# Late-used loads moved behind the first adaptive weights, and half of these weights put in operand slots, in a decoder trunk kernel

## Chip, core and metric

The kernel runs on one core of a Trainium2 chip. The metric is the device time of one launch in microseconds (us). A core has a tensor engine (PE, with its weight loads listed apart as PEld), a vector engine (DVE), a scalar engine (ACT), GpSimd (POOL), a sync engine (SP) that here issues nearly all loads, and 16 DMA engines that carry them out.

## What is computed

One sequence of 256 positions with 2048 features goes through two layers: an RWKV-7 time mix and a convolution module, each followed by a gated MLP. Each part is preceded by an RMS norm whose scale and shift come from a vector c. What bears on the change is the entry of the first layer:

```python
mod = silu(c) @ ada_w[0] + ada_b[0]          # 6 pieces of 2048: sh_m, sc_m, g_m, sh_f, sc_f, g_f
h  = rms_norm(x, g) * (1 + sc_m) + sh_m
xx = token_shift(h) - h
x_rkv = h + xx * mu[:3]                       # inputs of r, k, v
r, k, v = x_rkv @ w_rkv                       # three 2048 x 2048 products
xw, xa, xg = (h + xx * mu[n] for n in (3, 4, 5))
... tanh(xw @ w1), xa @ a1, sigmoid(xg @ g1)  # small inner products (widths 96, 96, 256)
```

Later stages use the rest of the parameters (biases, depthwise weights, gains), constant matrices, and silu(c) spread over all partitions for the other adaptive pieces, which the vector engine computes as row sums.

## The kernel before

Features lie on the 128 partitions, so a tensor of 2048 features is 16 tiles f = 0 to 15 of 128 x 256 positions. Weights come from memory in float32 in tiles of 128 x 2048 (1024 KB), and are split into a high and a low float32r part (`split_w`, L226: the high part by ACT at L231, the low by DVE at L232) for three matmuls each.

**Buffers.** Weights land in `raw_tile()`, a ring of four buffers. Operands live in `slot()`, a ring of 44 buffers of 2 x 260 columns; `slot512()` (L105) is one as a flat tile of 512 columns. The first stage fills the slots step by step: x takes 8, each tile leaves two operands and half of a third. The split weights have three buffers each.

**Head.** The sync queue first gets cb (c on all partitions, L168), all parameters par (L169), x in eight pieces (L332) and all constants cst (L333). ACT makes silu of cb; DVE makes three small derived vectors from par (L338 to L340); x is squared and summed for the norm.

**First stage**, lines 355 to 416. `ada_s(f)` computes scale and shift of tile f: it loads small weights lw (L359), then the adaptive weights in two halves `ada_s[f, 0]` and `ada_s[f, 1]`, each in a raw buffer (L364), for 16 matmuls with 32 columns (L367) into a PSUM tile of which one is free at a time, then loads the key weights w_k of tile f (L244). A copy on ACT (L371), two small products (L373) and two additions on DVE turn the sums into scale and shift. The loop then calls `ada_s(f + 1)`, scales tile f, mixes it with its shifted self for the different inputs, and makes ten key products with split weights (L398 to L400) and the inner products (L404 to L407). So a tile takes three raw buffers of the four: two halves and one w_k.

**What sets the order.** The code is traced; then a scheduler sorts the instructions of each engine's queue by its own estimate of readiness, and each queue runs in that order. A load that needs no buffer to come free can be placed far ahead of its place in the code. Buffers are handed out by the scheduler; a load into one waits until those who read its last content are done. The eight completion counters of loads are reused in turn, so a load also waits for the one eight places before it.

Of the kernel before, what the change touches and what calls it, by code (L numbers as in the profile page):

```python
# [14 lines left out]
ALU = mybir.AluOpType  # L15
# [65 lines left out]
SLAG = 2  # L81
BX = 2
CME = {mybir.EngineType.PE}
KAPPA = math.exp(-0.5)

_PCOLS = [
    ("gam_mix", 2 * KT), ("gam_ffn", 2 * KT), ("gam_fin", KT),
    ("ada_b", 2 * 6 * KT), ("c", KT), ("mu", 6 * KT),
    ("w0", KT), ("a0", KT), ("k_k", KT), ("k_a", KT), ("r_k", KT),
# [6 lines left out]
for _n, _w in _PCOLS:  # L96
    POFF[_n] = _o
    _o += _w
NPC = _o

_CCOLS = [("ident", P), ("bones", P), ("cen", P), ("ones", P), ("bo32", 32), ("sel", P),
          ("strict", T), ("incl", 2 * L), ("smask", T), ("eps", 4), ("e4", 1)]
COFF = {}
_o = 0
for _n, _w in _CCOLS:  # L105
    COFF[_n] = (_o, _w)
    _o += _w
NCC = _o


@with_exitstack
def trunk_kernel(ctx: ExitStack, tc: tile.TileContext, a, out):
# [24 lines left out]
    def raw_tile():  # L137
        return pool.tile([P, 2048], F32, tag="raw", bufs=4, name=nm("raw"))
# [22 lines left out]
    def act(o, i, func=AF.Identity, bias=0.0, scale=1.0):  # L161
        nc.scalar.activation(out=o, in_=i, func=func, bias=bias, scale=scale)  # L162

    # ---- constants, parameters
    cst = cp.tile([P, NCC], F32, name="cst")
    par = cp.tile([P, NPC], F32, name="par")
    cb = cp.tile([P, C], F32, name="cb")
    nc.sync.dma_start(out=cb, in_=a["cb"])  # L168
    nc.sync.dma_start(out=par, in_=a["par"])  # L169

# [4 lines left out]
    def pc(n, i=0, w=1):  # L175
        return par[:, POFF[n] + i:POFF[n] + i + w]
# [5 lines left out]

    act(cb, cb, AF.Silu)
    md = [cp.tile([P, 6 * KT], F32, name=f"md{i}") for i in range(2)]
# [37 lines left out]

    # ---- linear layers
    def split_w(r, k0, k1, step=1024, eng=None):
# [39 lines left out]
    class k_outer:  # L264
        """some outputs together, the operands fed one at a time; the weights split ahead, two operands' at once"""

# [39 lines left out]

    # ---- rms norm
    def sq_acc(st, x):
# [15 lines left out]

    # ================= layer 0: time mix =================
    hs = [slot() for _ in range(KT // 2)]
# [4 lines left out]
    for i in range(KT // 2):  # L331
        nc.sync.dma_start(out=hs[i][:, :, :T], in_=a["xT"][:, 2 * i:2 * i + 2, :])  # L332
    nc.sync.dma_start(out=cst, in_=a["cst"])  # L333
    st = [None]
# [3 lines left out]
    nc.vector.tensor_scalar(out=omu, in0=pc("mu", 0, 6 * KT), scalar1=-1.0, scalar2=1.0, op0=ALU.mult, op1=ALU.add)  # L338
    nc.vector.tensor_scalar(out=nkk_c, in0=pc("k_k", 0, KT), scalar1=-1.0, scalar2=None, op0=ALU.mult)
    nc.vector.tensor_scalar(out=oka, in0=pc("k_a", 0, KT), scalar1=-1.0, scalar2=1.0, op0=ALU.mult, op1=ALU.add)  # L340

    def xmix(n, f, t):
        act(t, hv(f), scale=omu[:, n * KT + f:n * KT + f + 1])
        stt(t[:, 1:T], hv(f)[:, 0:T - 1], pc("mu", n * KT + f), t[:, 1:T])
# [12 lines left out]
    def ada_s(f):  # L357
        lw = slot().rearrange("p a t -> p (a t)")[:, :448]
        nc.sync.dma_start(out=lw, in_=a["lw1"][f])  # L359
        # scale and shift of tile f  # L360
        pa = ps("y")
        for q in range(2):
            r = raw_tile()
            nc.sync.dma_start(out=r, in_=a["ada_s"][f, q])  # L364
            for k in range(8):
                g, kk = k % 4, 8 * q + k
                nc.tensor.matmul(pa[32 * g:32 * g + 32, :T], lhsT=cc[:, kk, :], rhs=r[:, k * T:(k + 1) * T],  # L367
                                 start=kk < 4, stop=kk >= 12, skip_group_check=True)
# [12 lines left out]
    for f in range(KT):  # L381
# [33 lines left out]
        xv32.append(xvp[-1][:, f % 2, :T])  # L415
        xmix(2, f, xv32[f])
    act(tw[:DL], lwa[:DL, :T], AF.Tanh)
    nc.scalar.copy(ta[:DL], lwa[:DL, T:])
# [17 lines left out]

    # ---- k, decay, a; A, B, K of the scan; N
    for f in range(KM, KT):
# [126 lines left out]

    # ---- inverse of the 32-blocks, all heads and chunks on partitions
    X = raw_tile()
# [65 lines left out]

    # ---- v, scan, group norm, bonus, gate
    def small(tag, w, bufs):
# [36 lines left out]
    def prep_gen(f):  # L672
# [7 lines left out]
        yield 0  # L680
        # products of A, R with B, K, and B, K by tokens
        for c in range(NC_):
# [12 lines left out]
            yield PU  # L695
        # off-diagonal block of the inverse
        py = ps("g")
# [5 lines left out]
        for h in range(2):  # L703
            r1 = slice(h * L + 32, h * L + 64)
            nc.scalar.copy(ysb[r1].rearrange("p c t -> p (c t)"), py[r1, :P])
        # bonus
        rk = t1()
# [6 lines left out]
        yield PU  # L714
        # centred V by tokens, in the other half of the partitions
        pvt = ps("g")
# [107 lines left out]

    # half of the output projection and residual, while the scan goes on
    def wo_gen(m):
# [34 lines left out]
    with tc.manual_schedule(engines={mybir.EngineType.PE}):  # L861
        while heap:
# [4 lines left out]
            if d is not None:  # L867
                at(t + d, g)
    # ---- output projection and residual
    # gain * x, with the shift in the last columns: the products of the two are rstd-free  # L870
    def operand(l, which, f):
# [29 lines left out]

    # ---- ConvGLU
    def ffn(l, st, ops, nops):
# [54 lines left out]

    # ================= layer 1: conformer convolution =================
    ops = nops  # L960
# [23 lines left out]

    # n of the taps on the tensor engine, m on GpSimd, the others on the vector engine in two chains
    def tap(f, d):
# [138 lines left out]

    # ---- final norm
    rstd = rstd_of(st)
# [108 lines left out]
```

## Time and profile before

| | us |
|---|---|
| median of 3 runs | 2667.47 |
| lowest, highest run | 2666.54, 2671.47 |
| span of the profiled execution | 2670.5 |
| PE busy in it | 2520.7 (94%) |
| DVE busy | 2003.9 (75%) |
| ACT busy | 1357.1 (51%) |

The profile is of one execution, whose span is the time from its first to its last instruction; a time of that execution beside its span is not listed. A busy PE need not be one at its peak. What is of use here are the first 200 us: how busy PE and the DMA engines are in stretches, what the sync queue waits for before it issues, how long a load takes from issue to landing, and the chain of work that ended last.

### The profile page before, as it was taken

The numbers are of one execution on the slowest core, as the hardware profiler recorded it, in microseconds if no ns is written. First come the engines' busy times: TensorE is split into PE (matmuls) and PEld (weight loads), VectorE is DVE, ScalarE is ACT, GpSimd is POOL, SyncE is SP. The second block draws the span as 40 slices with busy tenths as digits, with TensorE's granted clock in tenths as the row PEclk, the third lists the DMA queues.
The fourth block names the chain that finished last, engine by engine and source line by source line (L and its number), as shares of the span: only waits on it lengthen the run. The fifth ranks groups of instructions, "written<-read, shape, count | busy, mean of one in ns | idle before, by whom it ended". The sixth has DMA issues, their size and how long they took to land.

```text
span 2670.5 us, 52899 instructions
## 1 busy us (share of the span) xinstructions
PE 2520.7 (94%) x21250; PEld 2404.8 (90%) x21250; DVE 2003.9 (75%) x3635; ACT 1357.1 (51%) x2650; POOL 464.0 (17%) x452
## 2 busy tenths in 40 slices
PE   6899996999999999999999999978899999999998
PEld 3678885877799999999999999967899999999997
DVE  4567767768688888887878979979988656656665
ACT  4565622556555543553455555554555445534553
POOL 0000015544000012001100248954200000000000
PEclk9999997989999999999999999989999999999999
DMA  8887766677277778777978844436777655555553
GB/s 312 316 312 268 211 207 209 230 218 240 78 284 278 283 285 331 292 281 290 336 263 296 305 161 164 168 127 243 286 275 273 220 188 188 170 190 190 178 175 126
DMA packets 154805, 630.84 MB, mean 236 GB/s; under 512 B 60480, under 2 KB 72256, under 8 KB 95936
## 3 DMA queue, kind: packets, MB, share of 16 engines
q1 hardware_dynamic: 153824, 624.85, 65.9%
q8 instruction: 166, 2.72, 0.4%
q0 software_dynamic: 736, 2.62, 0.3%
q14 instruction: 79, 0.65, 0.1%
HBM read 614.30 MB, written 13.11 MB: 235 GB/s over the span
## 4 chain that ended last, share of the span: by engine, by line
PE 76%; DVE 10%; DMA 7%; ACT 3%; issue 2%; POOL 1%; SPq 0%; DVEq 0%; POOLq 0%; ACTq 0%
PE ps L237 22%; PE ps L239 22%; PE ps L238 21%; DMA raw<-ada 4%; DVE raw L208 3%; DVE s L159 2%; DVE lo L232 1%; PE ps L367 1%; PE ps L300 1%; DMA raw<-ada_s 1%; POOL lo L232 1%; DVE s L156 1%; PE ps L687 1%; ACT hi L231 1%; PE ps L398 1%
## 5 line engine op out<-in xcount | busy, mean ns | idle before, releaser
L237 PE MATMUL ps<-s,hi 128*128 128x258 f32 (+1 forms) x5584 | 1594.8, 286 | 7.5 <-ACT hi L231 6.4
L239 PE MATMUL ps<-s,lo 128*128 128x258 f32 (+1 forms) x5584 | 1581.6, 284 | 20.8 <-DVE lo L232 18.9
L238 PE MATMUL ps<-s,hi 128*128 128x258 f32 (+1 forms) x5584 | 1579.8, 283 | 0.6 <-DVE s L153 0.6
L231 ACT CAST hi<-raw 128x1024 fp32r<-128x1024 f32 (+6 forms) x873 | 769.7, 897 | 881.8 <-PE ps L238 606.1
L239 PEld LDWEIGHTS ps<-s,lo 128*128 128x128 f32 x5584 | 1063.7, 191 | 29.4 <-DVE lo L232 22.8
L237 PEld LDWEIGHTS ps<-s,hi 128*128 128x128 f32 x5584 | 1060.2, 190 | 16.8 <-ACT hi L231 8.6
L238 PEld LDWEIGHTS ps<-s,hi 128*128 128x128 f32 x5584 | 1063.4, 190 | 4.5 <-issue 3.0
L232 DVE TENSOR_TENSOR lo<-raw,hi 128x1024 fp32r<-128x1024 f32 (+4 forms) x639 | 746.0, 1171 | 303.5 <-ACT hi L231 301.8
L232 POOL TENSOR_TENSOR lo<-raw,hi 128x512 fp32r<-128x512 f32 x234 | 335.2, 1458 | 957.5 <-ACT hi L231 623.4
L208 DVE CUSTOM_DVE_ANT_0 raw<-raw,cb,par 128x1024 f32<-128x1024 f32 x156 | 213.2, 1367 | 76.0 <-DMA raw<-ada 71.3
L208 DVE CUSTOM_DVE_ANT_0 raw<-raw,cb,md 128x1024 f32<-128x1024 f32 x156 | 214.9, 1378 | 0.9
L159 DVE SCALAR_TENSOR_TENSOR s<-ps,par,s 128x239 f32<-128x239 f32 (+26 forms) x420 | 166.0, 456 | 1.8 <-ACT s L162 1.2
L1135 POOL TENSOR_TENSOR s<-s,t 128x256 f32<-128x256 f32 x6 | 4.1, 727 | 751.4 <-DVE t L322 751.4
L156 DVE TENSOR_TENSOR t<-ps,t 128x256 f32<-128x256 f32 x188 | 79.2, 422 | 47.5 <-PE ps L239 43.8
L159 DVE SCALAR_TENSOR_TENSOR s<-ps,md,s 128x256 f32<-128x256 f32 x117 | 55.9, 480 | 41.8 <-PE ps L239 41.7
L159 DVE SCALAR_TENSOR_TENSOR t<-t,par,t 128x255 f32<-128x255 f32 (+1 forms) x172 | 82.6, 480 | 1.9 <-ACT t L162 0.6
L156 DVE TENSOR_TENSOR s<-ps,cst 64x64 f32<-64x64 f32 (+2 forms) x208 | 48.1, 253 | 37.7 <-ACT n L689 27.0
L162 ACT ACTIVATE t<-t,par 128x256 f32<-128x256 f32 x118 | 68.1, 587 | 5.6 <-DVE t L156 2.5
L162 ACT ACTIVATE t<-t 128x256 f32<-128x256 f32 x102 | 42.5, 417 | 37.9 <-DVE t L159 24.1
L687 PE MATMUL ps<-s,s 128*128 128x128 f32 x256 | 46.6, 308 | 11.6 <-ACT s L694 10.6
L300 PE MATMUL ps<-s,raw 128*128 128x256 f32 x256 | 56.0, 380 | 0.0
L300 PEld LDWEIGHTS ps<-s,raw 128*128 128x128 f32 x256 | 48.4, 190 | 6.9 <-issue 0.3
(199 smaller groups left out, 2167.2 us busy)
## 6 DMA issues: line engine op xcount, KB each, us to landing
raw<-w_up SPq DMA_DIRECT2D x172, 1024.0 KB, 4.9
raw<-ada SPq DMA_DIRECT2D x156, 1024.0 KB, 6.7
raw<-w_dn SPq DMA_DIRECT2D x64, 896.0 KB, 4.7
raw<-w_pw SPq DMA_DIRECT2D x48, 1024.0 KB, 4.9
raw<-w_rkv SPq DMA_DIRECT2D x38, 1024.0 KB, 6.0
raw<-ada_s SPq DMA_DIRECT2D x32, 1024.0 KB, 6.4
raw<-w_dn SPq DMA_DIRECT2D x32, 960.0 KB, 4.9
raw<-w_o SPq DMA_DIRECT2D x11, 1024.0 KB, 4.9
```

The costliest lines, as they stand in the source:

```text
L156: nc.vector.tensor_tensor(out=o, in0=x, in1=y, op=ALU.mult)
L159: nc.vector.scalar_tensor_tensor(out=o, in0=x, scalar=s, in1=y, op0=op0, op1=op1)
L162: nc.scalar.activation(out=o, in_=i, func=func, bias=bias, scale=scale)
L208: nc.vector.tensor_tensor_reduce(out=r[q], in0=r[q], in1=cb[:, q * w:(q + 1) * w], scale=1.0, scalar=mod(l, piece, f) if q else pc("ada_b" ...
L231: nc.scalar.copy(hi[:, s], v[:, s])
L232: (eng or nc.vector).tensor_tensor(out=lo[:, s], in0=v[:, s], in1=hi[:, s], op=ALU.subtract)
L237: nc.tensor.matmul(acc[:, :n], lhsT=hi[:, c], rhs=x[:, 0, :n], start=first, stop=False)
L238: nc.tensor.matmul(acc[:, :n], lhsT=hi[:, c], rhs=x[:, 1, :n], start=False, stop=False)
L239: nc.tensor.matmul(acc[:, :n], lhsT=lo[:, c], rhs=x[:, 0, :n], start=False, stop=last)
L300: nc.tensor.matmul(acc[:, :T], lhsT=r[:, k * P:(k + 1) * P], rhs=hs32[k], start=k == 0, stop=k == n - 1)
L367: nc.tensor.matmul(pa[32 * g:32 * g + 32, :T], lhsT=cc[:, kk, :], rhs=r[:, k * T:(k + 1) * T], start=kk < 4, stop=kk >= 12, skip_group_che ...
L687: nc.tensor.matmul(pg[:, h * P:(h + 1) * P], lhsT=bkc, rhs=ari[h][:, c].rearrange("p j t -> p (j t)"), start=True, stop=True, skip_group_c ...
```

## The change

- The columns of par and cst are sorted anew, so that what the first stage uses stands first (336 of 1432 columns, 168 of 716 KB; 133 of 1317 columns, 66.5 of 658.5 KB). Only these are loaded at the head, and no cb.
- The rest of par and cst, and cb, are loaded by three instructions that stand in the code behind tile 13 of the first stage. The two derived vectors `nkk_c` and `oka` and the silu of cb stand behind the stage's loop.
- For tiles below SLF = 10, the second half of the adaptive weights goes to four slots of 512 columns, in four loads of 256 KB, instead of one raw buffer.

```diff
+SLF = 10
 _PCOLS = [
-    ("gam_mix", 2 * KT), ("gam_ffn", 2 * KT), ("gam_fin", KT),
-    ("ada_b", 2 * 6 * KT), ("c", KT), ("mu", 6 * KT),
+    ("gam_mix", 2 * KT), ("ada_b", 2 * 6 * KT), ("c", KT), ("mu", 6 * KT),
+    ("gam_ffn", 2 * KT), ("gam_fin", KT),
...
+NPE = POFF["gam_ffn"]
...
-    nc.sync.dma_start(out=cb, in_=a["cb"])
-    nc.sync.dma_start(out=par, in_=a["par"])
+    nc.sync.dma_start(out=par[:, :NPE], in_=a["par"][:, :NPE])
+    nc.sync.dma_start(out=cst[:, :NCE], in_=a["cst"][:, :NCE])
...
-    act(cb, cb, AF.Silu)
...
-    nc.sync.dma_start(out=cst, in_=a["cst"])
...
-            r = raw_tile()
-            nc.sync.dma_start(out=r, in_=a["ada_s"][f, q])
+            if q and f < SLF:
+                r = [slot512() for _ in range(4)]
+                for j in range(4):
+                    nc.sync.dma_start(out=r[j], in_=a["ada_s"][f, q][:, 2 * j * T:2 * (j + 1) * T])
+                r = [r[k // 2][:, (k % 2) * T:(k % 2 + 1) * T] for k in range(8)]
+            else:
+                r = raw_tile()
+                nc.sync.dma_start(out=r, in_=a["ada_s"][f, q])
+                r = [r[:, k * T:(k + 1) * T] for k in range(8)]
...
         xmix(2, f, xv32[f])
+        if f == KT - 3:
+            nc.sync.dma_start(out=par[:, NPE:], in_=a["par"][:, NPE:])
+            nc.sync.dma_start(out=cst[:, NCE:], in_=a["cst"][:, NCE:])
+            nc.sync.dma_start(out=cb, in_=a["cb"])
+    nc.vector.tensor_scalar(out=nkk_c, in0=pc("k_k", 0, KT), scalar1=-1.0, scalar2=None, op0=ALU.mult)
+    nc.vector.tensor_scalar(out=oka, in0=pc("k_a", 0, KT), scalar1=-1.0, scalar2=1.0, op0=ALU.mult, op1=ALU.add)
+    act(cb, cb, AF.Silu)
```

The order that the scheduler makes of it differs from the code's. In it the line numbers are those of each kernel: the issue of w_k is L244 before and L246 after, of ada_s L364 before, L369 (raw) and L365 (slot) after, of lw L359 and L358.

The sync queue of before, from the second half of tile 1 (`raw_213`) over the key weights of tile 1 (`raw_223`) and both halves of tile 2 (`raw_303`, `raw_313`) to the key weights of tile 3:

```order
L364 DMA raw_213<-ada_s 128x2048
L244 DMA raw_223<-w_k 128x1280
L364 DMA raw_303<-ada_s 128x2048
L364 DMA raw_313<-ada_s 128x2048
L244 DMA raw_323<-w_k 128x1280
L359 DMA s_300<-lw 128x448
L364 DMA raw_402<-ada_s 128x2048
L364 DMA raw_412<-ada_s 128x2048
L244 DMA raw_422<-w_k 128x1280
```

The same queue after, from the key weights of tile 1 (`raw_231`): first halves of tiles 2 and 3 are `raw_311` and `raw_416`, the first quarter of tile 2's second half is `s_321`, the two `l` are small weights of a later stage, which before stand two places ahead of `raw_213`:

```order
L246 DMA raw_231<-w_k 128x1280
L424 DMA par<-par 128x1096
L425 DMA cst<-cst 128x1184
L426 DMA cb<-cb 128x2048
L551 DMA l_418_2277<-lw 96x256
L551 DMA l_421_2285<-lw 96x256
L369 DMA raw_311<-ada_s 128x2048
L246 DMA raw_337<-w_k 128x1280
L369 DMA raw_416<-ada_s 128x2048
L358 DMA s_308<-lw 128x448
L365 DMA s_321<-ada_s 128x512
```

The three moved loads stand between tile 1 and tile 2, and the key weights of tile 2, the first half of tile 3 and lw of tile 2 have come ahead of the second half of tile 2.

The sync queue of before further on, with what each load waits for (PE, DVE: those that read the buffer's last content; DMAHW: the completion counters of loads): both halves of tile 6 are `raw_701` and `raw_711`, of tile 7 `raw_800` and `raw_810`:

```order
L364 DMA raw_701<-ada_s 128x2048 [waits DMAHW4_49,DMAHW1_49,PE_49]
L359 DMA s_598<-lw 128x448
L364 DMA raw_711<-ada_s 128x2048 [waits DMAHW2_49,PE_49]
L359 DMA s_698<-lw 128x448 [waits DMAHW7_49]
L244 DMA raw_721<-w_k 128x1280 [waits DMAHW0_49,DVE_49]
L364 DMA raw_800<-ada_s 128x2048 [waits DMAHW4_49,PE_49]
L364 DMA raw_810<-ada_s 128x2048 [waits DMAHW3_49,DVE_49]
L244 DMA raw_820<-w_k 128x1280 [waits DMAHW6_49,PE_49]
```

The same place after: key weights of tiles 6 and 7 are `raw_759` and `raw_864`, the first half of tile 7 is `raw_838`, the four quarters of tile 6's second half are `s_743` to `s_746`, the first half of tile 8 is `raw_944`:

```order
L246 DMA raw_759<-w_k 128x1280 [waits DMAHW2_49,PE_49]
L369 DMA raw_838<-ada_s 128x2048 [waits DMAHW3_49,DVE_49]
L246 DMA raw_864<-w_k 128x1280 [waits DMAHW4_49,PE_49]
L358 DMA s_730<-lw 128x448 [waits DMAHW5_49]
L365 DMA s_743<-ada_s 128x512 [waits DMAHW6_49]
L365 DMA s_744<-ada_s 128x512 [waits DMAHW7_49]
L365 DMA s_745<-ada_s 128x512 [waits DMAHW0_49]
L365 DMA s_746<-ada_s 128x512 [waits DMAHW1_49]
L369 DMA raw_944<-ada_s 128x2048 [waits DMAHW2_49,DVE_49]
```

The quarters wait for no buffer of their own, but stand behind the key weights of the next tile, which wait for PE; the buffer that these take is that of tile 6's first half.

The vector queue after, in tile 0 (`t_286` and `t_297` are mixes of it, `lo_353` is the low part of tile 1's key weights):

```order
L162 SCALAR_TENSOR_TENSOR t_286<-s_79,par,t_286 128x255
L427 TENSOR_SCALAR nkk_c<-par 128x16
L428 TENSOR_SCALAR oka<-par 128x16
L162 SCALAR_TENSOR_TENSOR t_297<-s_79,par,t_297 128x255
L234 TENSOR_TENSOR lo_353<-raw_231,hi_352 128x640
```

Before, `nkk_c` and `oka` were the second and third instruction of that queue; now they stand inside tile 0 and read the late part of par.

## Rows read from the trace of the kernel before

**Rows 1.** Busy time by stretch: engine columns in us with instructions, clock, DMA share, GB/s.

```profile
core 0: us, PE busy (x) PEld busy (x) DVE busy (x) ACT busy (x) POOL busy (x), PEclk, DMA share, GB/s
0.00:20.00 20.00, 2.31 (x14) 1.18 (x18) 7.87 (x19) 10.95 (x21) 0.73 (x5) 1.00 0.94 344
...
38.00:45.00 7.00, 7.00 (x57) 4.83 (x58) 0.83 (x2) 1.45 (x2) 0.00 (x0) 1.00 0.00 1
50.00:170.00 120.00, 106.58 (x939) 81.84 (x938) 61.78 (x159) 66.07 (x150) 0.00 (x0) 0.96 0.88 321
190.00:210.00 20.00, 20.00 (x170) 19.94 (x169) 16.02 (x22) 8.58 (x13) 0.00 (x0) 1.00 0.90 332
```

**Rows 2.** Waits of the sync queue, 0 to 330 us: us in total, times, longest.

```profile
SPq L364 <- PE ps L367: 50.5, 19, 10.9
SPq L364 <- DVE lo L232: 27.5, 8, 5.1
```

**Rows 3.** Timeline of the head: start us, length us, instruction, idle time before and its end.

```profile
5.70 1.91 ACT L162 ACTIVATE cb<-cb 128x2048 f32<-128x2048 f32 x1 [3.67 <-DMA cb<-cb]
...
8.38 0.72 ACT L162 ACTIVATE t<-s 128x256 f32<-128x256 f32 x2 [0.50 <-DMA s<-xT]
...
27.62 1.50 SPq L364 DMA_DIRECT2D raw<-ada_s  x2
...
34.79 1.44 PE L398 MATMUL ps<-s,hi 128*128 128x256 f32 x5 [1.28 <-ACT s L304]
```

**Rows 4.** Loads: KB, us to landing (issued 28.8; 44.9; medians, twice 0-300, once all).

```profile
raw<-ada_s SPq DMA_DIRECT2D x1, 1024.0 KB, 7.6
...
raw<-ada_s SPq DMA_DIRECT2D x1, 1024.0 KB, 4.7
...
raw<-w_k SPq DMA_DIRECT2D x16, 640.0 KB, 6.2
...
s<-lw SPq DMA_DIRECT2D x16, 224.0 KB, 6.6
...
s<-dT SPq DMA_DIRECT2D x64, 16.0 KB, 2.2
```

**Rows 5.** Chain that ended last, in order of time: start us, us, engine, tile, line.

```profile
54.38 1.04 PE ps L367 x16
...
65.57 1.04 PE ps L367 x16
66.64 0.38 ACT t L371
67.06 0.62 PE ps L373 x4
...
68.17 1.07 PE ps L367 x16
69.24 0.60 PE ps L404 x2
...
71.74 1.00 PE ps L367 x16
72.74 0.32 PE ps L399
...
75.89 0.34 PE ps L373 x4
...
144.90 0.34 PE ps L373 x4
```

**Rows 6.** Busy time of four stretches of 4 us, columns as in rows 1.

```profile
84.00:88.00 4.00, 1.00 (x12) 0.86 (x16) 3.31 (x11) 3.36 (x9) 0.00 (x0) 1.00 0.95 341
88.00:92.00 4.00, 4.00 (x26) 2.89 (x16) 0.00 (x0) 0.00 (x0) 0.00 (x0) 0.57 0.82 288
104.00:108.00 4.00, 2.04 (x32) 1.25 (x28) 3.15 (x10) 3.58 (x10) 0.00 (x0) 1.00 0.94 359
108.00:112.00 4.00, 4.00 (x33) 3.34 (x25) 0.70 (x2) 0.38 (x2) 0.00 (x0) 1.00 0.87 288
```

**Rows 7.** Busy time of the stretch with sixteen loads of 256 KB into slots.

```profile
1750.00:1768.00 18.00, 14.11 (x114) 13.88 (x113) 17.02 (x48) 10.74 (x29) 12.30 (x15) 1.00 0.80 264
```

**Rows 8.** Scan, 440-720 us: PE's waits for state updates (us, times); half reductions (min/median/max ns).

```profile
  PE ps L750: 6.2, 8
...
L208 DVE CUSTOM_DVE_ANT_0 raw<-raw,cb,md x32: 1267/1284/3492, 438.7 to 664.6; 128x1024 f32<-128x1024 f32 x32
```

More of the change, by code (lines that the diff above doesn't have):

```diff
@@ L99 @@
 NPC = _o
-_CCOLS = [("ident", P), ("bones", P), ("cen", P), ("ones", P), ("bo32", 32), ("sel", P),
-          ("strict", T), ("incl", 2 * L), ("smask", T), ("eps", 4), ("e4", 1)]
+NPE = POFF["gam_ffn"]
+_CCOLS = [("ones", P), ("eps", 4), ("e4", 1), ("ident", P), ("bones", P), ("cen", P), ("bo32", 32), ("sel", P),
+          ("strict", T), ("incl", 2 * L), ("smask", T)]
 COFF = {}
@@ L108 @@
 NCC = _o
+NCE = COFF["ident"][0]
 @with_exitstack
@@ L338, in trunk_kernel @@
     nc.vector.tensor_scalar(out=omu, in0=pc("mu", 0, 6 * KT), scalar1=-1.0, scalar2=1.0, op0=ALU.mult, op1=ALU.add)
-    nc.vector.tensor_scalar(out=nkk_c, in0=pc("k_k", 0, KT), scalar1=-1.0, scalar2=None, op0=ALU.mult)
-    nc.vector.tensor_scalar(out=oka, in0=pc("k_a", 0, KT), scalar1=-1.0, scalar2=1.0, op0=ALU.mult, op1=ALU.add)
     def xmix(n, f, t):
@@ L362, in ada_s @@
         for q in range(2):
-            r = raw_tile()
-            nc.sync.dma_start(out=r, in_=a["ada_s"][f, q])
+            if q and f < SLF:
[7 more added lines that the diff above has]
+                r = [r[:, k * T:(k + 1) * T] for k in range(8)]
             for k in range(8):
                 g, kk = k % 4, 8 * q + k
-                nc.tensor.matmul(pa[32 * g:32 * g + 32, :T], lhsT=cc[:, kk, :], rhs=r[:, k * T:(k + 1) * T],
+                nc.tensor.matmul(pa[32 * g:32 * g + 32, :T], lhsT=cc[:, kk, :], rhs=r[k],
                                  start=kk < 4, stop=kk >= 12, skip_group_check=True)
```

## The prediction

> **What bounds the kernel now.** I read the stretches of the first 210 us first [rows 1]. From 190 us on the tensor engine (PE) has no free time (20.00 of 20 us) and nothing later starts at a fixed time, so whatever the first stage saves or loses is passed on whole. In the first stage PE isn't full: 106.58 of 120 us from 50 to 170, with the DMA engines at 0.88 of their time and 321 GB/s, so 321 / 0.88 = 365 GB/s is what they move while busy. From 38 to 45 they move nothing at all: the next loads wait for raw buffers. The sync queue's waits say for what [rows 2]: 50.5 us until L367 has read an adaptive-weight half, 27.5 us until a w_k has been split. So two things bind, in turn: the head (loads until PE has work) and the ring of four raw buffers, three of which each feature tile needs. I call tile f's adaptive halves A(f) and B(f), its keys W(f), its small weights lw(f), and M(f) the end of its k products. In before M(1) ends at 54.38 and M(10) at 144.90 [rows 5]: 90.5 us for nine tiles, 10.06 each.
>
> **The change, part by part.**
>
> *The head.* Ahead of x there now stand 168 KB of parameters and 66.5 KB of constants in place of 1024 KB of cb and 716 KB of parameters; in before the first square waits until 8.38 and the first key product until 34.79 [rows 3]. About 1500 KB less at 2.7 us per 1000 KB (below) is 4 us, and 658.5 KB of constants leave the place behind x: some 5 to 7 us earlier for tile 0. But the three late loads (548 + 592 + 1024 = 2164 KB) are not late. They wait for no buffer, and in the built program they stand right behind W(1) and ahead of A(2). So the sum up to there is as before, and W(2), A(3) and lw(2) (640 + 1024 + 224 = 1888 KB [rows 4]) now stand ahead of B(2) as well. In before B(2) is the second issue of 27.62 + 1.50 [rows 3], at 28.8, and lands 7.6 later, at 36.4 [rows 4]. Ahead of it and with it went 12510 KB (cb, parameters, x, constants, two lw, six halves, two w_k, two small loads); the first issue at 0.74 and a least landing time of 2.2 (16 KB, [rows 4]) leave 33.5 us for them, 2.68 per 1000 KB. With 1888 KB more B(2) lands at 36.4 + 5.1 = 41.5. Tile 0's products lie in that wait, so the 5 to 7 us are not gained: M(1) hangs on B(2).
>
> *What follows a B.* From the chain [rows 5]: B ends at 66.61, A of the next tile at 69.24: 2.6 us for the copy on ScalarE, the small products, the add that frees the PSUM tile, and A itself. Products of a tile: 69.24 to 71.74 and 72.74 to 75.89, 5.65 us. So M(1) = 41.5 + 0.3 (the last pair of B) + 2.6 + 5.65 = 50.1. PE has then idled from about 36 to 41, and after such a stretch it has mostly run at the lower of its two levels (1.2 of 2.4 GHz): granted 0.57 in 88 to 92, behind a stretch with 1.00 of 4 us busy [rows 6]. A drop then costs up to 4 x 0.43 = 1.7 us. I take it whole: M(1) = 51.8, against 54.38.
>
> *The slots.* For f below 10 each tile takes two raw buffers instead of three. In the built program A and W are then a whole tile further ahead. But B(f) isn't, for f = 4, 6, 7, 8, 9: it stands behind W(f+1), and that waits until PE has read A(f), whose buffer it takes. On the in-order sync queue lw(f), the four quarters of B(f) and all behind them wait with it. From A's end then: 2.2 until something lands, 640 + 224 + 1024 KB = 1.93 MB at 365 GB/s = 5.3, 0.3, and 2.6 to the next A's end: a period of 10.4. PE has 5.65 of products to cover it, so it waits some 2 us each time. For f = 3 and 5 the quarters are queued early and the period is PE's own: 5.65 + 1.04 + 2.6 = 9.3. Behind A(10) stands a whole B(10), ahead of B(9): 2.2 + 2.33 MB / 365 = 6.4, + 0.3 + 2.6, + 1.04 for B(10), 12.5. M(9) comes 6.0 later (0.34 + 5.65), M(10) after A(11), B(11) and a chain, 2.1 + 2.6 + 5.65 = 10.3. M(2) to M(10): 61.1, 71.5, 80.8, 91.2, 101.6, 112.0, 124.5, 130.5, 140.8. Against 144.90 that is a gain of 4.1. Before's 90.5 us held three drops of the clock; I allow the new run one more besides the restart, 1.7, since it waits in five short pieces instead of three long ones. That leaves 2.4 at M(10). Behind it all three loads of a tile use raw buffers as before, and from A(14) the sync queue stands as before: nothing, plus or minus 1.5.
>
> *Other moves.* Vector work on the late parameters stands in tile 0 ahead of its last mixes: at 2.68 per 1000 KB the parameters (8650 KB with all ahead of them) land near 26, the queue gets there near 27 (34.79 less the 5 to 7), and tile 0 has until 41. ScalarE's Silu of cb (1.91 us [rows 3], and a table load) stands behind tile 0's mixes and waits for cb (10270 KB, near 30); the second half of W(1)'s split stands behind it, which M(1) needs only after 44. Both cost nothing, as long as B(2) is late; were B(2) on time, they would cost up to 2 us. The 32 more issues on the sync queue lie in its waits. In the scan later, PE's order is the same, but 16 of 64 state updates on the vector engine, in three stretches, have one more half reduction ahead (1284 ns [rows 8]): between 0 and 3 x 1.3 = 3.9 us. PE waits for these updates 6.2 us in 8 waits from 440 to 720 [rows 8], 0.8 each; I take one of them, 0.8, and not less than 0, as nothing moves off that path for good.
>
> Sum: 4.1 - 1.7 - 0.8 = 1.6 us. The span is 2670.5, 3.0 above the median and inside the spread of the runs; the difference is carried to the median: 2667.5 - 1.6 = 2665.9.
>
> **The rivals.**
>
> *Faster: DMA catches up.* Where the queue is empty before a load, 1024 KB land in 4.7 [rows 4], 2.5 without the 2.2: 420 GB/s, and in the new order the queue is often empty when W(f+1) is issued. The period of 10.4 is then 9.7, four times, and 0.8 less for A(10); with no further drop of the clock and no lag in the scan: 1.6 + 2.8 + 0.8 + 1.7 + 0.8 = 7.7, 2659.8. For it: 2.04 busy of 4 us in 104 to 108 was followed by 1.00 [rows 6]. Against it: 365 GB/s is what 120 us of just this traffic show.
>
> *Slower: the clock.* The new waits are short, but come in nearly every tile. If PE falls to the lower level after each of M(2) to M(8), that is seven times 1.7 in place of one: 10.2 lost against 1.6, 2676.1. It decides from two drops on, where 4.1 - 0.8 is used up. For it: B, the small products and the waits round them leave PE at 1.6 to 2 busy of 4 us. Against it: the same 2.04 of 4 without a drop [rows 6].
>
> *Slower: quarters.* Sixteen loads of 256 KB in rows of 2 KB run in 1750 to 1768 at 264 GB/s [rows 7]. At that pace a B takes 4.0 instead of 2.9, exposed six times (B(2), four periods, B(9)): 6.6 lost against 1.6, 2672.5. The Trainium skill ("DMA: Bandwidth & Descriptors", Bandwidth) asks for loads of 1 MiB or more, and by it quartering speaks against the change. Against the rival: that stretch has the DMA engines at 0.80 only, and the quarters here stand in one queue with others behind and ahead.
>
> *It doesn't do what it says* is half of the forecast: the late loads move by two tiles, not to the end. Had they stood behind B(13), B(2) would land 5.8 earlier; the built order excludes it.
>
> **How the numbers follow.** The forecast 0.50, alone 2661 to 2671 (the scan's 0 to 3.9, the end's 1.5, one drop more or less); faster by DMA 0.28; clock 0.15; quarters 0.07. What a measurement can tell from no change is about 0.2%, 5.3 us: 2662.1 to 2672.8. Faster: 0.25 of the first rival and 0.08 of the forecast's low end, 0.33. Slower: 0.14 of the clock, 0.04 of the quarters and 0.01, 0.19. Same: 0.48. Range: 2657 to 2674, which leaves out the clock's upper half and a tenth of the faster case.
>
> **What would show it.** Right: the three late loads issued between 18 and 26 us; DMA busy without a gap to 45; B(2) landing near 41 and PE nearly idle before; sync waits of L246 (w_k) for PE, then PE waiting about 2 us for the quarters at f = 4, 6, 7, 8, 9; M(1) near 52, M(10) near 140 to 142. Wrong: M(10) before 137 (then the wait for the quarters isn't there), or granted clock below 0.9 over 55 to 125 (the clock's rival), or a difference that arises after 190 us (then the scan's order weighs more than the first stage).

## The result and the profile after

The change made the kernel slower: 2692.03 us median (2689.17 to 2694.82) against 2667.01 us of before measured beside it, a ratio of 1.0092 (95% interval 1.0078 to 1.0106). The forecast was 2665.9 us with a range of 2657 to 2674. The profiled run took 2694.82 us, its span 2692.7 us; 22 us of the loss lie between the two profiled spans.

The stretches of the first 140 us after the change, with the columns of [rows 1], and one row each for the whole first stage of after (to its last key product, at 203.3 us) and of before (183.5 us):

```profile
20.00:38.00 18.00, 13.09 (x94) 9.15 (x94) 10.67 (x32) 9.61 (x18) 0.00 (x0) 0.81 1.03 386
38.00:45.00 7.00, 3.10 (x16) 0.75 (x16) 0.83 (x1) 0.72 (x1) 0.00 (x0) 0.63 1.03 408
...
60.00:80.00 20.00, 16.94 (x122) 11.79 (x120) 6.83 (x17) 6.85 (x14) 0.00 (x0) 0.83 0.77 247
...
100.00:120.00 20.00, 13.96 (x107) 8.38 (x110) 7.72 (x21) 8.61 (x20) 0.00 (x0) 0.91 0.65 244
120.00:140.00 20.00, 16.89 (x114) 11.01 (x104) 9.73 (x25) 10.20 (x25) 0.00 (x0) 0.74 0.63 218
...
0.00:203.30 203.30, 156.20 (x1184) 111.31 (x1185) 99.26 (x250) 103.67 (x225) 0.73 (x5) 0.89 0.79 282
```

```profile
0.00:183.50 183.50, 143.97 (x1184) 107.60 (x1185) 98.65 (x250) 101.20 (x220) 0.73 (x5) 0.97 0.85 313
```

The gap of DMA from 38 to 45 us [rows 1] is filled, 1.03 instead of 0.00. But from 60 us on the DMA engines are busy 0.63 to 0.77 of the time instead of 0.88, so over the stage they have time to spare; inside the waits that are shown below they haven't. The two last rows split the stage's 19.8 us more: the same 1184 products keep PE busy 156.20 us instead of 143.97 (12.2 us, all but 0.2 of it in the adaptive products), and PE is idle 47.1 us instead of 39.5 (7.6 us).

What SP waits for after the change, 0 to 330 us (us in total, times, longest), against [rows 2]:

```profile
SPq L246 <- PE ps L373: 35.1, 10, 7.0
SPq L369 <- DVE lo L234: 30.2, 9, 5.5
SPq L369 <- PE ps L373: 27.1, 8, 8.7
```

The wait for PE's reads of the adaptive halves has gone in good part from the halves themselves (L364 before, L369 now) to the key weights (L246), and the quarters of a second half stand behind these. What that does is in the chain that ended last; two tiles of it, to be read as [rows 5] (L373 are the adaptive products, L377 and L379 what follows a second half, L365 the issue of the quarters):

```profile
57.57 1.10 PE ps L373 x16
...
59.55 6.70 DMA s<-ada_s
...
66.29 3.00 PE ps L373 x16
...
69.74 1.03 PE ps L379 x4
...
71.12 1.93 PE ps L373 x16
...
81.57 1.10 PE ps L373 x16
...
82.69 0.33 SPq L246
...
83.08 0.42 SPq L358
...
83.54 0.43 SPq L365
...
84.01 5.99 DMA s<-ada_s
...
90.04 0.63 PE ps L373 x4
...
90.67 0.63 PE ps L373 x4
...
91.30 0.65 PE ps L373 x4
...
91.97 0.38 ACT t L377
...
92.40 0.62 PE ps L379 x4
...
93.50 1.10 PE ps L373 x16
```

At 82.67 PE has read A(6). Only then is W(7) issued, lw(6) and the quarters of B(6) behind it; the quarters land one after the other until 91.3, and A(7) is read at 94.6: a period of 11.9 us, 9.3 of them from the end of A to the end of B. PE's products cover only part of that. The timeline of the same tile (start us, length us), and the stretch of the wait with the columns of [rows 1]:

```profile
83.54 2.14 SPq L365 DMA_DIRECT2D s<-ada_s  x4
...
88.06 0.33 SPq L369 DMA_DIRECT2D raw<-ada_s  x1
...
89.34 2.58 PE L373 MATMUL ps<-s,s 128*32 128x256 f32 x16 [1.28 <-DMA s<-ada_s]
...
93.50 1.07 PE L373 MATMUL ps<-raw,s 128*32 128x256 f32 x16 [0.50 <-PE ps L379]
```

```profile
82.67:91.30 8.63, 7.28 (x50) 5.34 (x51) 3.72 (x8) 3.14 (x7) 0.00 (x0) 1.00 0.91 294
```

The sync queue is busy with the issues of W(7), lw(6) and the quarters until 85.68. In the wait the DMA engines are busy 0.91. And since each quarter is read as it lands, the sixteen products of B(6) keep PE busy 2.58 us, those of A(7) behind them 1.07, both at a granted clock of 1.00. In the earlier tile the wait was followed by the lower clock as well: the sixteen products of B(4) took 3.00 us and those of A(5) 1.93, and the granted clock of 66 to 70 and 70 to 74 us is 0.64 and 0.50.

Of the wait for quarters the rows on L373's idle time speak (us, times):

```profile
  DMA s<-ada_s: 39.4, 33
```

To compare kernels I use four marks. M(1) and M(10) are counted from windows that begin at 0 (ten key products per tile, to half a us). The other marks are the first or last start of a line: the last key product (L404 after), the first L701 of the scan, the last L812, the gate's product. For after these rows give 203.3, 432.5 and 748.7:

```profile
L404 PE MATMUL ps<-s,hi x160: 276/281/775, 29.3 to 203.3; 128*128 128x256 f32 x160
...
L701 PE MATMUL ps<-cst,s x128: 275/275/421, 432.5 to 719.4; 128*128 128x128 f32 x128
...
L812 PE MATMUL ps<-tg,g x64: 378/379/796, 563.3 to 748.7; 128*128 128x256 f32 x64
```

"Stage one" is the time to the last key product, "second" from there to the scan's first product, "scan" to the last gate product, "rest" what remains of the span. All in us, one profile per row:

| kernel | M(1) | M(10) | stage one | second | scan | rest | span |
|---|---|---|---|---|---|---|---|
| before | 54.0 | 144.5 | 183.5 | 230.1 | 308.6 | 1948.3 | 2670.5 |
| before, 2nd profile | 53.0 | 145.0 | 184.0 | 230.1 | 302.3 | 1945.6 | 2662.0 |
| before, 3rd profile | 52.0 | 140.5 | 180.0 | 230.1 | 307.1 | 1946.9 | 2664.1 |
| after | 54.5 | 158.5 | 203.3 | 229.2 | 316.2 | 1944.0 | 2692.7 |
| after, 2nd profile | 55.5 | 155.0 | 196.0 | 230.5 | 320.2 | 1937.3 | 2684.0 |
| head alone | 54.5 | 139.0 | 183.4 | 230.9 | 312.9 | 1946.2 | 2673.4 |
| slots alone | 51.0 | 156.5 | 198.9 | 231.1 | 317.1 | 1944.1 | 2691.2 |
| quarters, no slots | 53.0 | 147.5 | 190.4 | 229.1 | 314.2 | 1950.0 | 2683.7 |
| quarters on GpSimd's queue | 66.0 | 149.5 | 192.3 | 230.7 | 304.0 | 1947.4 | 2674.4 |
| late loads held back | 48.5 | 155.0 | 197.4 | 229.1 | 311.3 | 1943.5 | 2681.3 |
| quarters a tile ahead | 53.5 | 131.0 | 173.7 | 232.4 | 314.2 | 1947.1 | 2667.4 |
| both, held to tile 13 | 51.5 | 126.0 | 169.4 | 240.0 | 299.9 | 1946.6 | 2655.9 |
| both, held to tile 6 | 52.5 | 132.0 | 174.5 | 230.0 | 311.0 | 1939.0 | 2654.5 |
| the same, all 16 tiles | 55.0 | 139.0 | 181.9 | 230.1 | 306.5 | 1946.8 | 2665.3 |
| before, vector order by hand | 52.0 | 135.5 | 175.5 | 229.4 | 317.1 | 1969.9 | 2691.9 |
| after, vector order by hand | 54.0 | 152.5 | 196.4 | 229.5 | 318.2 | 1963.2 | 2707.3 |
| both, held to tile 6, vector order by hand | 51.0 | 131.0 | 173.7 | 230.3 | 310.2 | 1970.0 | 2684.2 |

The last three belong to the section on the scan; the first of them runs stage one in before's order, so before's stage one is seen to spread from 175.5 to 184.0. On the means of the two profiles of after and the three of before, stage one is 199.7 against 182.5 (+17.2), the scan 318.2 against 306.0 (+12.2), the rest 1940.7 against 1946.9 (-6.3): +22.8 us of span, for 25.0 between the medians. So two stages lose.

### The profile page after: what moved, and what is told of

Its sections match the earlier page's. It is cut to its first block, busy times and chain, and to the rows that moved or that the text cites. A ratio compares the mean times of both kernels' runs of the same rounds, so it can differ in the third digit from the quotient of the medians.

```text
span 2692.7 us, 52937 instructions
## 1 busy us (share of the span) xinstructions
PE 2535.5 (94%) x21250; PEld 2408.9 (89%) x21250; DVE 2001.2 (74%) x3635; ACT 1356.4 (50%) x2651; POOL 466.8 (17%) x452
## 4 chain that ended last, share of the span: by engine, by line
PE 74%; DVE 11%; DMA 10%; issue 2%; ACT 2%; POOL 1%; SPq 1%; DVEq 0%; ACTq 0%; POOLq 0%
PE ps L241 22%; PE ps L239 22%; PE ps L240 21%; DMA raw<-ada 4%; DVE raw L210 4%; DVE s L162 2%; DMA s<-ada_s 1%; PE ps L373 1%; DVE lo L234 1%; DVE s L159 1%; DVE raw L153 1%; DMA s<-dAR 1%; DVE s L210 1%; PE ps L812 1%; DMA raw<-ada_s 1%
## 5 line engine op out<-in xcount | busy, mean ns | idle before, releaser
L210 DVE CUSTOM_DVE_ANT_0 raw<-raw,cb,par 128x1024 f32<-128x1024 f32 x156 | 211.7, 1357 | 83.7 <-DMA raw<-ada 80.4
L210 DVE CUSTOM_DVE_ANT_0 raw<-raw,cb,md 128x1024 f32<-128x1024 f32 x156 | 214.8, 1377 | 1.1
L159 DVE TENSOR_TENSOR t<-ps,t 128x256 f32<-128x256 f32 x188 | 79.2, 422 | 47.3 <-PE ps L241 40.4
L159 DVE TENSOR_TENSOR s<-ps,cst 64x64 f32<-64x64 f32 (+2 forms) x208 | 48.0, 253 | 36.4 <-ACT n L702 26.2
L162 DVE SCALAR_TENSOR_TENSOR t<-s,par,t 128x255 f32<-128x255 f32 x80 | 35.0, 479 | 44.3 <-ACT t L165 44.3
```

The lines of the kernel that those rows point to most:

```text
L159: nc.vector.tensor_tensor(out=o, in0=x, in1=y, op=ALU.mult)
L162: nc.vector.scalar_tensor_tensor(out=o, in0=x, scalar=s, in1=y, op0=op0, op1=op1)
L210: nc.vector.tensor_tensor_reduce(out=r[q], in0=r[q], in1=cb[:, q * w:(q + 1) * w], scale=1.0, scalar=mod(l, piece, f) if q else pc("ada_b" ...
```

## The experiments

Theories: *queue* (second halves stand behind key weights that wait for PE), *pace* (quarters move slower), *head* (the three loads that come early push tiles 1 and 2 back), *scan* (moved vector work costs by itself).

### One part alone

The head of the change without slots:

```diff
-SLF = 10
+SLF = 0
```

> The head of the changed kernel alone: the split parameters and constants, the broadcast vector and its Silu as in the change, but no half of the adaptive weights in free slots. The scheduler puts the three late loads (2.2 MB) behind tile 1's first half and ahead of its second. Queue theory (the loss of 25 us comes from the second halves that stand on SP behind the next tile's key weights, which wait for PE): nothing of it is here, the end of tile 10's k products stays at 143 to 147 us (144.90 before) and the time at 2664 to 2670. Head theory (the three late loads push tile 1 and 2 back and the stage never recovers): the second stage begins 5 to 20 us later than the 184.1 of before, time 2672 to 2687. Scan theory (the moved vector work in the scan costs by itself): stage one as before, scan 5 to 8 us longer, time 2672 to 2675.

2679.68 us against 2670.44, ratio 1.0032 (1.0012 to 1.0051). Stage one ends at 183.4 as in before, with M(10) at 139.0 a little earlier than I expected: the head alone neither gains nor costs there, and the head theory falls. The time is still some 8 us up, above the 2675 that the scan theory allowed; the scan, at 312.9, holds 4 to 11 of them.

The slots without the head (the kernel before, and this):

```diff
-            r = raw_tile()
-            nc.sync.dma_start(out=r, in_=a["ada_s"][f, q])
+            if q and f < SLF:
+                r = [slot512() for _ in range(4)]
+                for j in range(4):
+                    nc.sync.dma_start(out=r[j], in_=a["ada_s"][f, q][:, 2 * j * T:2 * (j + 1) * T])
...
```

> The other half alone: the head as before, second halves of tiles 0 to 9 in four 128x512 loads into free slots. Queue theory: second halves stand again behind the next tile's key weights, first half to first half takes 11 to 14 us as in the changed kernel instead of about 9.5; the end of tile 10's k products comes at 153 to 162 us (144.90 before, 158.86 after), time 2680 to 2695. Head theory: periods as before, tile 10 done at 143 to 147, time 2664 to 2670.

2695.14 us, ratio 1.0101 (1.0071 to 1.0131): as much as the whole change, with M(10) at 156.5. Stage one's loss is the slots', not the head's. The scan, 317.1, is as long as after's although no vector work has moved in this kernel, so the scan theory fails as it was put. The two halves of the change (8 us and 24) don't add up to its 25.

### Queue or pace

The quarters into the raw buffer that one load filled:

```diff
-            nc.sync.dma_start(out=r, in_=a["ada_s"][f, q])
+            if q and f < SLF:
+                for j in range(4):
+                    nc.sync.dma_start(out=r[:, 2 * j * T:2 * (j + 1) * T], in_=a["ada_s"][f, q][:, 2 * j * T:2 * (j + 1) * T])
+            else:
+                nc.sync.dma_start(out=r, in_=a["ada_s"][f, q])
```

> The kernel before with one edit: the second half of tiles 0 to 9 is loaded by four loads of 128x512 into the same raw buffer that one load filled, so they wait for the same reader and stand in the place of the one. Queue theory: no change but the issues of thirty more loads (about 0.7 us for each group on SP, beside transfers), tile 10 done at 143 to 148 us, time 2664 to 2672. Pace theory: the second halves move at 220 to 265 GB/s instead of 365, 1.0 to 1.9 us more for each of ten tiles, tile 10 done at 153 to 162 us, time 2677 to 2692.

M(10) at 147.5 is the queue theory's, but the time, 2685.54 us and 1.0053 (1.0028 to 1.0078), is the pace theory's. Stage one ends 6 to 10 us after before's; some 4 of them arise behind M(10) (42.9 us from there on, 39.0 to 39.5 in before), where no tile is quartered. The scan is 314.2. M(10) itself is 2.5 to 7.0 us later than in the three profiles of before. So four pieces aren't free: a group takes 1.75 to 2.92 us to issue on SP between 55 and 120 us, one whole half 0.33, and I had expected 0.7 more. Whether issue or pace costs these few us, and what lengthens the tiles behind, I didn't settle.

The changed kernel with the quarters on another queue:

```diff
-                    nc.sync.dma_start(out=r[j], in_=a["ada_s"][f, q][:, 2 * j * T:2 * (j + 1) * T])
+                    nc.gpsimd.dma_start(out=r[j], in_=a["ada_s"][f, q][:, 2 * j * T:2 * (j + 1) * T])
```

> The changed kernel with one edit: the forty quarter loads are issued on the GpSimd queue instead of SP, so that none of them stands behind a key-weight load that waits for PE. Queue theory: the quarters of the first tiles are issued at once and the later ones when a slot comes free; the period falls from 9.6 to 16.2 us to 9 to 11, tile 10 is done at 135 to 147 us, time 2660 to 2675. Pace theory (loads of 256 KB with 2 KB rows move at 220 to 265 GB/s wherever they stand): the period stays at 11 to 14, tile 10 done at 153 to 162 and time 2685 to 2695. Scan theory: even with stage one healed the scan stays some 7 us longer than before, time 2670 to 2675.

2674.71 us, ratio 1.0024 (1.0009 to 1.0039). No adaptive product waits for a quarter any more (39.4 us in after), and from M(2) at 77.0 to M(8) at 132.0 a tile takes 9.2 us, against 13.2 in after (64.0 to 143.0) and 9.75 in before (65.5 to 124.0). The head pays: the quarters of the first tiles are issued at once and compete with x, whose pieces take 13.9 us to land instead of 4.8 (medians), so the first key product comes at 47.7 instead of 29.3. That is why M(10), 149.5, lies 2.5 past what I expected.

The same queue, the same pieces, but written one tile ahead, so that the scheduler sets B(f) before the load that waits for A(f):

```diff
+    def quarters(f):
+        if f < SLF:
+            qs[f] = [slot512() for _ in range(4)]
+            for j in range(4):
+                nc.sync.dma_start(out=qs[f][j], in_=a["ada_s"][f, 1][:, 2 * j * T:2 * (j + 1) * T])
+
     def ada_s(f):
+        if f == 0:
+            quarters(0)
+        quarters(f + 1)
...
-                r = [slot512() for _ in range(4)]
-                for j in range(4):
-                    nc.sync.dma_start(out=r[j], in_=a["ada_s"][f, q][:, 2 * j * T:2 * (j + 1) * T])
+                r = qs.pop(f)
```

> The changed kernel with the quarter loads written one tile ahead in the code (those of tile f+1 before the first half of tile f), same pieces, same SP queue, three late loads hoisted as in the change. The scheduler then puts the quarters of tile f ahead of the load that waits for PE's read of tile f's own first half. Queue theory: periods of 9 to 10 us, tile 10 done at 138 to 147 us (158.86 after), last key product at 178 to 186 (203.3 after), time 2662 to 2672. Pace theory: as after within 5 us, 2685 to 2695. Scan theory: 2670 to 2675, with a last gate product 314 to 318 us after the first product of the scan (308.6 before, 316.2 after).

M(10) at 131.0 and the last key product at 173.7, 22 to 30 us before after's, 2 to 10 before before's, and some 5 earlier than even the queue theory had it. The edit asks for the same loads on the same queue, only earlier, so this decides between queue and pace. The rows for 55 to 130 us and for the whole stage, columns as in [rows 1]:

```profile
55.00:130.00 75.00, 69.24 (x633) 56.27 (x632) 42.02 (x107) 44.42 (x99) 0.00 (x0) 0.98 0.91 328
...
0.00:173.70 173.70, 138.95 (x1183) 108.67 (x1184) 99.58 (x250) 103.56 (x225) 0.73 (x5) 0.98 0.91 330
```

and what PE's adaptive products of this kernel waited for, with no line for quarters among them:

```profile
  DMA raw<-ada_s: 10.0, 4
```

With the same 256 KB pieces the DMA engines are busy 0.91 of 55 to 130 us and move 328 GB/s, 360 while busy; [rows 1] give 365 with whole halves, after 339 (251 at 0.74). The Trainium skill ("DMA: Bandwidth & Descriptors", Bandwidth) asks for loads of 1 MiB or more; in these runs the smaller pieces cost a tenth of the pace at most over such a stretch. Yet the time is 2664.81 us, ratio 1.0003 (0.9985 to 1.0020): of the 9.8 us that this profile gains in stage one on the first of before, it gives 5.6 back in the scan (314.2) and 2.3 in the second stage.

### The head, with and without the queue

The late loads made late, by a write to each destination from a value of tile 13:

```diff
+            for d in (par[:, NPE:NPE + 1], cst[:, NCE:NCE + 1], cb[:, 0:1]):
+                nc.scalar.copy(d, x0[:, 0:1])
             nc.sync.dma_start(out=par[:, NPE:], in_=a["par"][:, NPE:])
```

> The changed kernel with the three late loads held back for real: ScalarE first writes one column of each destination from a value of tile 13, so their issue cannot move ahead of it (three one-column copies more). The second halves still stand behind the next tile's key weights. Queue theory: the first tiles gain (tile 1's k products end at 49 to 53 us instead of 55), then the periods of 12 to 14 us come back, tile 10 is done at 150 to 157 us, time 2682 to 2691. Head theory (the hoisted loads of 2.2 MB are what cost the 20 us of stage one): tile 10 at 138 to 147, time 2660 to 2672.

2682.62 us, ratio 1.0044 (1.0019 to 1.0070). M(1) falls from 55 to 48.5 as the queue theory said, and M(10) is at 155.0 all the same: what the early loads take from tile 1 is 6 to 7 us, and the periods behind it eat it.

Both edits:

> Both edits: quarters one tile ahead and the late loads held back to tile 13. Queue theory with the head's delay on top: tile 1's k products end at 46 to 52 us, last key product at 174 to 183 us, time 2656 to 2667. Pace theory: 2680 to 2695. Head theory: as the run with the late loads held back alone.

Stage one ends at 169.4, the earliest of all. The time is 2663.88 us, ratio 0.9990 (0.9973 to 1.0008). Held to tile 13, the loads come late for the second stage, which is 10 us longer. The chain between the two stages:

```profile
166.39 1.28 ACT L165
167.69 1.92 ACT cb L165
...
170.13 1.28 ACT L165
...
172.17 0.40 ACT t L446
172.61 0.38 PE ps L239
```

The Silu of cb stands on ScalarE ahead of what the second stage's first product needs: 1.92 of the 10 us. The two table loads of 1.28 us beside it have their like in before, ahead of the tanh and the sigmoid of this place. The other 8 us fall later in that stage, where I did not follow them; the next run shows that they hang on how late the loads are.

Held back to tile 6:

```diff
-        if f == KT - 3:
+        if f == 6:
```

> Quarters one tile ahead and the late loads held back to tile 6 instead of 13, so that the Silu of the broadcast vector (1.92 us on ScalarE, which stood ahead of the second stage with tile 13) lies inside the stage. Queue theory: last key product at 168 to 174 us, second stage 229 to 233 us long again (240.0 with tile 13), and 10 us of the stage reach the end: time 2653 to 2661. Scan theory (what stage one gains, the scan takes back): scan 312 to 318 us, time 2661 to 2668.

The second stage is back at 230.0, stage one at 174.5, half a us past what I expected. 2664.60 us against 2672.11 on that chip, ratio 0.9979 (0.9959 to 0.9999): at the very edge faster than before, and by the two ratios (0.9979 and 1.0092) 1.1% below the change. The time lies in the range of the scan theory, not of the queue theory; the scan, 311.0, is 2 to 9 us longer than in the profiles of before.

All sixteen tiles in slots (`SLF = 16`):

> The same with the second halves of all sixteen tiles in slots instead of ten. Queue theory: tiles 10 to 15 keep the period of 8 to 9.5 us, last key product at 163 to 172 us, time 2650 to 2660. Slot theory (slots are short at the stage's end, where four quarters wait for PE): last key product at 170 to 178 us, no better than with ten, 2655 to 2668.

Stage one ends at 181.9, 7 us worse than with ten and worse than both theories had it, and why I did not follow; the time is that of ten tiles: 2664.43 us, ratio 0.9986 (0.9965 to 1.0006).

### The scan

Another profile of after and two of before, for the spread:

> The changed kernel once more, for the spread between profiles of one kernel: stage one's last key product within 2 us of 203.3 and the scan (first product of it to the last gate product) within 3 us of 316.2, if the differences between kernels are larger than the spread; if the scan comes out 5 us or more apart, the scan's difference to before is no finding.

> The kernel before once more, for the spread between profiles. If the scan's 7.6 us more after (308.6 to 316.2, and 320.2 in the second profile) is an effect of the change, this scan lasts 306 to 311 us; if it is spread, 304 to 318. Stage one's last key product again at 181 to 186 us.

> The kernel before a third time, the same question: scan 306 to 311 us if the change made it longer, anywhere in 304 to 318 if it is spread.

Before's scan is 302.3 to 308.6, after's 316.2 and 320.2: no overlap, though the spread of 6 us is more than I allowed. Stage one spreads more, 196.0 and 203.3 for after.

Where after's scan falls behind can be counted on L701, eight products for each tile. From the seventh to the eighth tile it takes 30 and 26 us in the two profiles of after, 22, 22 and 22 in those of before: 4 to 8 of the 12 us. The chain there, and two stretches of it:

```profile
546.38 9.27 DMA raw<-ada
...
555.68 1.28 DVE raw L210
...
558.88 6.58 DMA raw<-ada
...
565.50 1.28 DVE raw L210
...
566.82 2.17 DVE raw L210
...
569.03 0.43 DVE t L159
...
569.50 2.08 PE ps L812 x4
```

```profile
568.00:572.00 4.00, 2.50 (x7) 2.14 (x8) 1.90 (x5) 0.98 (x3) 3.57 (x3) 0.61 0.49 173
572.00:576.00 4.00, 4.00 (x13) 2.28 (x13) 0.85 (x2) 1.65 (x6) 0.40 (x1) 0.50 0.50 172
```

Half reductions (L210) wait on VectorE for their weights, the gate's multiplication (L159) stands behind them, PE's gate products (L812) wait for it, and the granted clock falls to its lower level behind the wait.

Whether the order on VectorE is the cause: in the scan TensorE's order is written by hand, VectorE's is the scheduler's. This writes it by hand too, in before, in after, and in the version held back to tile 6:

```diff
-    with tc.manual_schedule(engines={mybir.EngineType.PE}):
+    with tc.manual_schedule(engines={mybir.EngineType.PE, mybir.EngineType.DVE}):
```

> The kernel before with one edit: in the scan the order of VectorE, too, is the order in which the code is written (TensorE's already is), so that the scheduler's choice there no longer depends on the stages ahead. Its scan may come out longer or shorter than the 302 to 309 us of before; it is the partner of the next run. Time 2650 to 2700.

> The changed kernel with the same edit: VectorE's work in the scan now stands in the same order as in the partner. Order theory (the scan's 12 us more come from half reductions that the scheduler set elsewhere on VectorE): the two scans are equal within 4 us, stage one stays 13 to 20 us longer than the partner's, and the time is 10 to 18 us above the partner's instead of 25. Other-cause theory (orders of ScalarE and SP, or what stage one leaves behind): this scan stays 8 us or more longer than the partner's and the time 20 us or more above.

> Quarters one tile ahead, late loads held back to tile 6, and VectorE in the scan in written order. Order theory: the scan is as long as the partner's within 4 us, so that the 8 to 10 us that stage one gains reach the end: time 6 to 12 us below that of the kernel before with the same edit.

First and last products of the scan in the first two, L688 and L799 in before's version, L701 and L812 in after's:

```profile
L688 PE MATMUL ps<-cst,s x128: 274/275/421, 404.9 to 686.5; 128*128 128x128 f32 x128
...
L799 PE MATMUL ps<-tg,g x64: 377/379/796, 531.7 to 722.0; 128*128 128x256 f32 x64
```

```profile
L701 PE MATMUL ps<-cst,s x128: 275/275/421, 425.9 to 706.2; 128*128 128x128 f32 x128
...
L812 PE MATMUL ps<-tg,g x64: 377/379/796, 554.2 to 744.1; 128*128 128x256 f32 x64
```

The scans are 722.0 - 404.9 = 317.1 and 744.1 - 425.9 = 318.2, equal within 1.1 us. Stage one still differs by 20.9 us (175.5 and 196.4), the spans by 15.4, the medians by only 8.3 (2697.30 and 2705.57), a little less than I expected. So with one order on VectorE the scan's difference is gone, in one profile of each. The written order itself is a bad one: 1.0110 (1.0066 to 1.0153) and 1.0140 (1.0087 to 1.0192) of before, with some 23 us more behind the scan. The third, 2691.81 us and 1.0091 (1.0062 to 1.0120), lies 5.5 us below its partner, just short of the 6 to 12 expected, and its scan is 310.2 although VectorE's order is the partner's: some 7 us of a scan's length don't come from that order.

The traces hold a second comparison. Read by their start times, VectorE's 560 instructions in the scan of the kernel with quarters on GpSimd's queue stand in before's order but for one, and ScalarE's too but for one. Its code for the scan is after's and its stage one ends at 192.3, yet the scan takes 304.0 us, among before's. In the kernel with both edits, held to tile 13, eight of VectorE's instructions are out of before's order, and the scan takes 299.9. In after 36 of 566 are, in the other kernels of the table that leave the order to the scheduler 22 to 57, and their scans take 306.5 (all 16 tiles) to 320.2. So before's order goes with a short scan, whatever came ahead of it, and another order in most kernels with a longer one.

## Why the prediction was wrong, point by point

*The head.* Right in the mechanism: the three loads went out at 18.8 to 21.9 us and DMA had no gap to 45. Of size: the quarters of B(2) landed at 41.8 to 44.7, not at 41.5, and their sixteen products took 3.1 us, with 0.63 granted from 38 to 45. M(1) came at 54.97 in the chain, 3.2 later than forecast, no earlier than the 54.38 of [rows 5]. That the early loads are the cause of M(1)'s lateness, the run that held them back shows (48.5).

*The period behind W(f+1).* This is the step that failed, by its size. I had the queue right: second halves behind key weights that wait for PE's read of A(f). But I priced the period at 10.4 us, 7.8 of them from A's end to B's end, with 1.93 MB at 365 GB/s. These 7.8 us measured 9.3 for tile 6 and 10.2 to 10.8 for tiles 4, 7, 8 and 9. Three things stand in them that the sum had not. I had put the more issues into the queue's waits, at nothing, but W(7), lw(6) and the four quarters take SP from 82.69 to 85.68, inside the wait. The 1.93 MB don't have the DMA engines to themselves: from 82.67 to 91.30 the engines move 294 GB/s, that is 2.54 MB, with the end of A(7), which lands at 83.7, and the beginning of A(8), issued at 88.06. And B's products come quarter by quarter, so that the last of them end 0.65 us behind the last landing and not 0.3. How the excess divides between the first two, no run isolates; that the place in the queue is what exposes it, the quarters a tile ahead show, with a period of 9.5. The periods of A(4) to A(10) were 14.4, 9.6, 11.9, 12.8, 13.1 and 16.2 in place of 10.4, 9.3, 10.4, 10.4, 10.4 and 12.5: 14.6 us more, of the 18.1 by which M(10) missed 140.8.

*The clock.* I took one further drop and gave the rival with seven a chance of 0.15 and 10 us. PE was busy 12.2 us longer with the same products (8.4 in the second profile, 152.34), but that is not all the clock's. The products of B(6) and B(7) ran at a granted 1.00 and kept PE busy 2.58 and 2.57 us in place of 1.07, for want of quarters. If the other four halves that PE waited for, B(2), B(4), B(8) and B(9), with 3.0 to 3.1 us each, owe as much to that, some 9 of the 12.2 us are this and not the clock (an estimate, 6 x 1.5). In the second profile B(4) and B(8) ran at 1.00 too, with 2.55 and 2.58 us, so there some 6 of the 8.4 us came at the full clock. The wait and the clock aren't two cases, as I had them: behind some of the waits the lower clock came (at 66 us, 114, 126 and 180), behind others not (90 and 103), and where it came it lengthened the period further. Nor is the price 1.7 us each: behind the wait for B(9) it stayed at the lower level from 130 to 138, granted 0.50. My mark for it, a clock below 0.9 over 55 to 125 us, was too coarse: the mean over 55 to 130 is 0.92.

*Quarters.* Rightly held unlikely as a matter of pace; the quarters' place in the queue was the cost, and their issue and their landing one by one a part of what it exposed.

*Behind M(10).* Forecast as nothing, plus or minus 1.5; it took 41.0 and 44.8 us in the two profiles, 43.9 with the vector order by hand, against 39.0 to 40.0 in four of before's order. So it wasn't nothing, but 1 to 6 us; the wait at 180, with a granted 0.50 from 182 to 186, is one place of it in the first profile.

*The scan.* The term 0 to 3.9 us, of which I took 0.8, was mis-sized: 12.2 us on the means. I counted half reductions of 1284 ns set ahead of state updates [rows 8]. What cost was that half reductions wait for their weights, so what stands behind them waits for a load, and then PE for the gate, and then the clock. The two kernels with one vector order, and the two other kernels whose order is nearly before's, make the order the cause of most of the difference. It isn't shown for all of it, since scans with one order on VectorE differ by up to 8 us, and which of the moved instructions cost it, no run isolates.

*Sum.* The forecast had 1.6 us gained. Stage one lost 17.2, the scan 12.2, and the rest gave 6.3 back, for which I have no cause.

*That everything behind 190 us passes the first stage's gain on whole* fell as well: with the quarters a tile ahead stage one ended 2 to 10 us earlier than in before's profiles and the time hardly moved.

## What to carry to other kernels

When a load gets a free buffer, ask what its in-order queue puts ahead of it: a load that waits for nothing is as late as the last waiting load before it, and the period must be priced with its issues and with every other load that is in flight then. Writing such loads one tile ahead moved them past the waiting ones and turned a loss of some 17 us in the stage into a gain of some 8 (172.8 on the mean of the four kernels with ten tiles a tile ahead, 180.8 on four profiles of before's order). Busy time of PE that grows isn't the clock by itself: look at the granted clock of the very products. A scheduler that plans from modelled times reorders stages that the diff doesn't touch; compare their length in more than one profile of each kernel before a gain or loss is put down to the stage that was edited.

## What the runs showed that I had not expected

One program's stages differ between profiles by 4 to 9 us (stage one of after 203.3 and 196.0, of before's order 175.5 to 184.0, before's scan 302.3 to 308.6), with single runs of before from 2655.64 to 2683.61 us; a difference in one stage of less than that needs a second profile. And waits of PE that look alike in the windows are followed by different clocks: with 2.09 of 4 us busy in 62 to 66 the granted clock fell to 0.64 and 0.50 for the next 8 us, with 2.03 of 4 in 98 to 102 it stayed at 1.00. Not even the kernel decides it: the same wait for B(4), 2.20 us in the first profile of after and 2.29 in the second, was followed by different clocks. The stretch behind it in the first, then in the second:

```profile
66.00:70.00 4.00, 3.24 (x18) 0.93 (x18) 0.00 (x0) 0.69 (x3) 0.00 (x0) 0.64 1.03 361
```

```profile
66.00:70.00 4.00, 2.50 (x16) 0.58 (x16) 0.48 (x1) 0.13 (x1) 0.00 (x0) 1.00 1.03 371
```

What tells the two apart the windows don't show.
